# Two FFN stages: the first unit's product P6 goes between P1 and P2, and the second unit's first low block is computed on VectorE

## Chip, cores and metric

One core of a Trainium2 chip runs the whole program. The metric is the device time of one execution in microseconds (us); of the kernel before, three runs and one profiled execution are shown. Less is better.

## What is computed

One layer of a hybrid decoder trunk on 512 tokens of width 1024, in float32: a half-step SwiGLU FFN, a token mixer (dilated attention beside an mLSTM), and a second half-step FFN, each between RMSNorms.

```
def swiglu(x, w_gate, w_up, w_down):
    return (jax.nn.silu(x @ w_gate) * (x @ w_up)) @ w_down
...
x = x + 0.5 * rmsnorm(swiglu(rmsnorm(x, ffn1_pre_g), ...), ffn1_post_g)
x = x + rmsnorm(hybrid_mixer(rmsnorm(x, mix_pre_g), ...), mix_post_g)
x = x + 0.5 * rmsnorm(swiglu(rmsnorm(x, ffn2_pre_g), ...), ffn2_post_g)
```

D_FF is 2816, that is 22 blocks of 128 columns. The change touches only the first product pair of the two SwiGLU blocks, `x @ w_gate` and `x @ w_up`.

## The kernel before

**Precision.** A float32 matrix is split in a high part (a cast to float32r, done by ScalarE) and a low part (the matrix minus its high part). A product is the sum of high x high, high x low and low x high.

**Units.** In each FFN stage (tiles with _a in the first, _b in the second), the first three blocks of 128 columns (f = 0, 1, 2; `PLAIN = 3`) are done in the plain way. The 19 others are the units of `seven` (line 313). For each of them, gate and up weights together form a 2 x 2 matrix of blocks, as does the input, and the four block products are formed by seven, P1 to P7, with sums of blocks before and after (the Strassen-Winograd scheme). `product(out, k, ...)` (line 358) is P_k: twelve matmuls, eight high and four low for k of 1 and 2 (moving tile 128x256), four high (128x512) and four low (128x256) for the others. All lie on line 368 in the profile. The order of TensorE's products is written out by hand and chained (`pe`), and the `Order` object `do` (line 273) chains the instructions that go through it, engine by engine, in the order of the code. So an instruction of ScalarE, VectorE or GpSimd that waits holds up all that are chained behind it. These instructions all have line 279 in the profile.

**Accumulators.** Each unit has a PSUM tile `qa` (P1, then P2 added onto it) and a tile `qbc` of two banks: b takes P6, then P7 and P4, and c takes P5, then P3. P1 alone is needed too, so ScalarE copies it from `qa` to `q1` (in the profile q) before P2 is added. VectorE then reads the two banks in `outer` (with P6 and P5 in them, two additions into z and uv) before P7 and P3 are added, and in `inner` after them.

**Weights of a unit.** `load` (line 321) fetches gate and up weights as two tiles g and u of 512 KB from SP's queue, three buffers in turn for all of them. So the load of u of unit n+1 overwrites the buffer of g of unit n, and waits for the last reader of that. `sums` forms four sums of blocks on VectorE (ab and cd), `take` makes high and low parts:

- wh, the high part, is a cast on ScalarE, for pairs of blocks: (1, 2) is g itself, (6, 3) is cd, (7, 5) is ab, (4) is half of u.
- wl, the low part, is made in one of two ways. For sums it is a VectorE subtraction, which `take` returns as a function, to be called where its place is. For stored blocks, g and half of u, ScalarE writes the negated high part into wl, and an adding DMA from GpSimd's queue adds the stored block onto it.

`front` (line 343) is the `take` for (1, 2). The first unit's uses the subtraction, all others the adding DMA.

**The start of a stage.** Both first units are loaded and their `front` is called; the first unit's other parts follow at once. In the loop's first turn there is no unit before (`prev` is None), and the products come in this order: P1, P2, P6, P5 of the first unit, P1 of the second, then P7 and P3 of the first. ScalarE's copy to q1 stands after P1, its silu of `qa` after P2. In the following turns a unit has P1 (the second unit's is done already), P6, P5, then P4 of the unit before, P2, P7, P3.

Of the kernel before, what the change touches and what calls it, by code (L numbers as in the profile page):

```python
# [39 lines left out]
def tile_hybrid_block(ctx: ExitStack, tc: tile.TileContext, a: dict):  # L40
# [272 lines left out]
    def seven(do, fs, wgu, x, low, scr, pairs, aT, name, ahead):  # L313
# [3 lines left out]
        class Unit:  # L317
# [23 lines left out]
                do("gpsimd", "dma_start", wl, stored, accum_op=ADD)  # L341

            def front(self):
                if self.f > fs[0]:
                    return self.take((1, 2), self.gu[0], 2, self.stored(0))
                self.take((1, 2), self.gu[0])()

            def sums(self):
                g, u = self.gu
# [55 lines left out]
        us = [Unit(f) for f in fs] + [None, None]  # L405
        for u in us[:2]:
            u.load()
            u.front()
            if u is us[0]:
                u.sums()  # L410
                u.lowcd()
                u.take((4,), u.gu[1][:, 1:2, :], 1, u.stored(1)[:, 1:2, :])
                u.take((7, 5), u.ab)()
        prev = None
        for i in range(len(fs)):
            u, v, w = us[i:i + 3]
            if i != 1:
                u.open()
            if prev:
                prev.inner()  # L420
                prev.silu(1)
            if not v:
                next(ahead)
            if i != 1:
                u.product(u.a, 1, True, False)
                cast(u.q1, u.a)
            if not prev:
                u.product(u.a, 2, False, True)
                u.silu(0)
            u.product(u.b, 6, True, False)  # L430
            if w:
                w.load()
            if v:
                v.sums()
            u.product(u.c, 5, True, False)
            u.outer()
            if v:
                v.lowcd()
            if prev:
                prev.finish()  # L440
            if v:
                v.take((4,), v.gu[1][:, 1:2, :], 1, v.stored(1)[:, 1:2, :])
            if prev:
                u.product(u.a, 2, False, True)
            else:
                v.open()
                v.product(v.a, 1, True, False)
                cast(v.q1, v.a)
            if v:
                lowab = v.take((7, 5), v.ab)  # L450
            else:
                next(ahead)
            if prev:
                u.silu(0)
            if v:
                lowab()
            u.product(u.b, 7, False, False)
            u.product(u.c, 3, False, True)
            if w:
                w.front()  # L460
            prev = u
# [11 lines left out]
    def halves(v, n):  # L473
        return v.rearrange("p (a b) -> p a b", b=n)

    class Down:
# [81 lines left out]
        def cast(self, s, which):  # L558
            v = self.src[s][which == "w"]
            pool, tag, n = (wpool, "w", WMAX) if which == "w" or not self.xp else (self.xp, "x", T)  # L560
            n_ = v.shape[1] * v.shape[2]
            hl = [pool.tile([P, n], F32R, tag=f"{tag}{y}", bufs=5, name=f"{which}{y}{s}_{self.name}")[:, :n_] for y in "hl"]
            self.do("scalar", "copy", halves(hl[0], v.shape[2]), v)
            (self.w if which == "w" else self.x)[s] = hl
# [87 lines left out]
    def ffn(pool, todo, first_w, hT, wgu, wdq, wdh, wd, post, finish, name, begin=None, pins=(), aT=None):  # L652
# [23 lines left out]
        for f in range(EARLY, PLAIN):  # L676
# [5 lines left out]
            for b in range(2):  # L682
# [8 lines left out]
        pairs = pctx.enter_context(tc.tile_pool(name=f"pairs_{name}", bufs=2, space=bass.MemoryType.PSUM,  # L691
                                                reuse_waits="tile"))
        last = seven(do, range(PLAIN, NF), wgu, x, low, scr, pairs, aT, name, ahead)
        dn = ExitStack()
        next(ahead)
# [1146 lines left out]
```

## Time and profile before

| what | value |
|---|---|
| median of three runs | 1310.59 us (1307.78 to 1311.33) |
| profiled execution, its own time | 1308.08 us |
| its span, from the first to the last instruction | 1306.3 us |
| granted TensorE clock | 0.999 |
| TensorE matmul busy | 1293.5 us, 99% of the span |
| VectorE busy | 1041.2 us, 80% |
| ScalarE busy | 722.8 us, 55% |
| GpSimd busy | 188.5 us, 14% |
| first FFN stage: starts of the first and last matmul of line 368 | 46.5 us and 240.3 us |
| second FFN stage: the same | 1003.2 us and 1195.8 us |

In the rows of the profile PE is TensorE's matmuls, PEld its weight loads, DVE is VectorE, ACT ScalarE, POOL GpSimd and SP the engine whose queue issues the loads. A row of a timeline has the start in us from the start of the span, the duration, engine, line, operation, output and inputs, the number of instructions merged in it, and in brackets the idle time of the engine before it and what ended that. Ends of matmuls are modelled, so the difference of two starts is the better measure of a product's length. The times of the runs and of the profiled execution are those of the whole execution, a little longer than the span.

### The profile page before, as it was taken

To read this page: it belongs to the slowest core of one execution; us is meant where nothing else is said; L and a number is where in the kernel's file an instruction comes from. 1 tells how busy PE (TensorE), PEld (TensorE's weight loads), DVE (VectorE), ACT (ScalarE), POOL (GpSimd) and SP (SyncE) were. 2 spreads that over 40 slices of the span, in tenths; PEclk is the share of its full clock that TensorE was granted. 3 is DMA by queue.
4 is the path that set the end of the run, shared out by engine and by line. 5 is a ranking of instruction groups with operands and counts; after the bars stand their busy time and mean duration, and the time that the engine had idled before them with its cause. 6 is when DMAs were issued, how large, how long until landed. Compare 5 with 4: busy or idle time off the path is not lost.

```text
span 1306.3 us, 19592 instructions
## 1 busy us (share of the span) xinstructions
PE 1293.5 (99%) x7413; PEld 1137.4 (87%) x7413; DVE 1041.2 (80%) x1601; ACT 722.8 (55%) x1139; POOL 188.5 (14%) x249
## 2 busy tenths in 40 slices
PE   9999999999999999999999999999999999999997
PEld 8899999888898888888888889999888999998886
DVE  7799998889894577576798687676388999998887
ACT  6566666566644546435565554434265666665663
POOL 1111111221302110011112010000010111111220
PEclk9999999999999999999999999999999999999999
DMA  5587888697468963257637532335414778876981
GB/s 196 127 200 181 185 193 187 179 241 157 149 174 191 327 129 116 73 159 177 218 90 179 169 97 65 98 113 162 162 61 110 192 176 191 193 178 176 271 171 65
DMA packets 62766, 211.49 MB, mean 162 GB/s; under 512 B 7316, under 2 KB 8364, under 8 KB 62416
## 3 DMA queue, kind: packets, MB, share of 16 engines
q0 software_dynamic: 29824, 94.06, 34.5%
q1 hardware_dynamic: 32832, 116.18, 27.2%
q8 instruction: 58, 0.95, 0.3%
q14 instruction: 36, 0.29, 0.1%
q10 hardware_dynamic: 16, 0.00, 0.0%
HBM read 200.70 MB, written 9.46 MB: 161 GB/s over the span
## 4 chain that ended last, share of the span: by engine, by line
PE 93%; issue 3%; DVE 2%; DMA 1%; ACT 1%; POOL 0%; POOLq 0%; DVEq 0%; ACTq 0%
PE qbc_b L368 10%; PE qbc_a L368 10%; PE pq L204 8%; PE pm L204 7%; PE qa_b L368 4%; PE qa_a L368 4%; PE qb_gm L1262 4%; PE acc_o L259 3%; PE accb_b L584 3%; PE vo1p L993 3%; PE w12p L993 3%; PE vo0p L993 3%; PE accb_a L584 3%; PE accc_b L584 2%; PE accc_a L584 2%
## 5 line engine op out<-in xcount | busy, mean ns | idle before, releaser
L368 PE MATMUL qbc_b<-x_b,wh_b 128*128 128x512 f32 x304 | 83.1, 395 | 0.0
L368 PE MATMUL qbc_a<-x_a,wh_a 128*128 128x512 f32 x304 | 83.1, 395 | 0.0
L204 PE MATMUL pq<-hT_mx,wh_qk 128*128 128x512 f32 x320 | 76.9, 392 | 0.0
L204 PEld LDWEIGHTS pq<-hT_mx,wh_qk 128*128 128x128 f32 x320 | 59.4, 188 | 12.0
L204 PE MATMUL pm<-hT_mx,wh_mqk 128*128 128x512 f32 x256 | 61.3, 392 | 0.0
L368 PEld LDWEIGHTS qbc_b<-x_b,wh_b 128*128 128x128 f32 x304 | 52.1, 189 | 7.0
L368 PEld LDWEIGHTS qbc_a<-x_a,wh_a 128*128 128x128 f32 x304 | 52.1, 189 | 7.0
L279 POOL DMA_DIRECT2D wl_a<-in_wgu x37 | 32.2, 869 | 176.8 <-ACT wl_a L279 144.3
L279 POOL DMA_DIRECT2D wl_b<-in_wgu x37 | 31.5, 851 | 173.1 <-ACT wl_b L279 135.4
L204 PEld LDWEIGHTS pm<-hT_mx,wh_mqk 128*128 128x128 f32 x256 | 47.4, 188 | 9.5
L368 PEld LDWEIGHTS qbc_b<-x_b,wl_b 128*128 128x128 f32 x304 | 46.6, 188 | 6.5
L368 PEld LDWEIGHTS qbc_a<-x_a,wl_a 128*128 128x128 f32 x304 | 46.6, 188 | 6.5
L368 PE MATMUL qbc_a<-x_a,wl_a 128*128 128x256 f32 x304 | 48.2, 280 | 0.0
L368 PE MATMUL qbc_b<-x_b,wl_b 128*128 128x256 f32 x304 | 48.2, 280 | 0.0
L368 PE MATMUL qa_a<-hT_f,wh_a 128*128 128x256 f32 x304 | 42.6, 283 | 0.7 <-ACT q_a L279 0.7
L368 PE MATMUL qa_b<-hT_f,wh_b 128*128 128x256 f32 x304 | 42.6, 283 | 0.5 <-ACT q_b L279 0.5
L114 DVE TENSOR_TENSOR wl_qk<-wf_qk,wh_qk 128x1024 fp32r<-128x1024 f32 x24 | 29.2, 1220 | 17.3 <-ACT wh_qk L98 9.3
L368 PEld LDWEIGHTS qa_a<-hT_f,wh_a 128*128 128x128 f32 x304 | 39.1, 190 | 1.0 <-ACT q_a L279 0.9
L368 PEld LDWEIGHTS qa_b<-hT_f,wh_b 128*128 128x128 f32 x304 | 39.1, 190 | 0.7 <-ACT q_b L279 0.7
L98 ACT CAST wh_qk<-wf_qk 128x1024 fp32r<-128x1024 f32 x24 | 25.0, 1046 | 26.3 <-PE pq L204 10.0
L204 PE MATMUL pq<-hT_mx,wl_qk 128*128 128x512 f32 x160 | 39.5, 389 | 0.0
L1170 DVE SCALAR_TENSOR_TENSOR z<-pm,cw,z 128x511 f32<-128x511 f32 (+2 forms) x48 | 35.3, 743 | 2.2 <-ACT z L1168 1.8
(955 smaller groups left out, 3855.2 us busy)
## 6 DMA issues: line engine op xcount, KB each, us to landing
wf_qk<-in_wqk SPq DMA_DIRECT2D x24, 512.0 KB, 4.4
g_a<-in_wgu SPq DMA_DIRECT2D x19, 512.0 KB, 5.4
u_a<-in_wgu SPq DMA_DIRECT2D x19, 512.0 KB, 5.4
g_b<-in_wgu SPq DMA_DIRECT2D x19, 512.0 KB, 5.5
u_b<-in_wgu SPq DMA_DIRECT2D x19, 512.0 KB, 5.2
wl_a<-in_wgu POOLq DMA_DIRECT2D x18, 512.0 KB, 5.6
wl_b<-in_wgu POOLq DMA_DIRECT2D x18, 512.0 KB, 5.6
wf_mqk<-in_wmqk SPq DMA_DIRECT2D x16, 512.0 KB, 4.3
```

Source lines behind the costliest of these rows:

```text
L98: return nc.scalar.copy(wh, wf)
L114: last_low[0] = nc.vector.tensor_tensor(wl[:, :m], wf[:, :m], wh[:, :m].bitcast(F32), op=ALU.subtract).ins
L204: nc.tensor.matmul(out, lhsT=wt[:, k * P:(k + 1) * P], rhs=x[:, k, 0:T], start=n == 0, stop=n == len(terms) - 1)
L259: nc.tensor.matmul(out, lhsT=x[:, tk], rhs=w[:, cs], start=first and n == 0, stop=last and n == 2, skip_group_check=True)
L279: self.last[eng] = getattr(getattr(nc, eng), fn)(*args, **kw).ins
L368: i = nc.tensor.matmul(o, lhsT=w, rhs=v, start=first and n == 0, stop=last and n == len(terms) - 1, skip_group_check=True)
L584: nc.tensor.matmul(o, lhsT=x[:, tk], rhs=w[:, cs], start=k in "1256" and g + m + n == 0, stop=False, skip_group_check=True)
L993: nc.tensor.matmul(out[k][i], lhsT=x[:, 2 * g + m, i * P:(i + 1) * P], rhs=y[:, m * T:(m + 1) * T], start=k in "156" and g + m + j == 0, s ...
L1170: nc.vector.scalar_tensor_tensor(z[:, s:], src[:, :T - s], cw[:, ct, 3 - s:4 - s], z[:, s:], op0=ALU.mult, op1=ALU.add)
L1262: nc.tensor.matmul(out, lhsT=wt[:, i * P:(i + 1) * P], rhs=y[:, i, :], start=first and m == 0, stop=last and m == len(terms) - 1, skip_gro ...
```

## The change

In the first turn of the loop, P6 of the first unit goes between its P1 and P2. The second unit's low block for P1 and P2 is now computed like the first one's, by a VectorE subtraction; that subtraction is placed behind the second unit's four sums, ahead of P5 and of `outer`. From the third unit on, the adding DMA stays. Both FFN stages call the same function, so it is changed in both.

```
             def front(self):
-                if self.f > fs[0]:
+                if self.f > fs[1]:
                     return self.take((1, 2), self.gu[0], 2, self.stored(0))
-                self.take((1, 2), self.gu[0])()
+                return self.take((1, 2), self.gu[0])
...
         for u in us[:2]:
             u.load()
-            u.front()
+            second = u.front()
             if u is us[0]:
+                second()
                 u.sums()
                 u.lowcd()
...
             if i != 1:
                 u.product(u.a, 1, True, False)
                 cast(u.q1, u.a)
+            u.product(u.b, 6, True, False)
             if not prev:
                 u.product(u.a, 2, False, True)
                 u.silu(0)
-            u.product(u.b, 6, True, False)
             if w:
                 w.load()
             if v:
                 v.sums()
+            if not prev:
+                second()
             u.product(u.c, 5, True, False)
             u.outer()
```

More of the change, by code (lines that the diff above doesn't have):

```diff
@@ L343, in front @@
             def front(self):
-                if self.f > fs[0]:
+                if self.f > fs[1]:
                     return self.take((1, 2), self.gu[0], 2, self.stored(0))
-                self.take((1, 2), self.gu[0])()
+                return self.take((1, 2), self.gu[0])
             def sums(self):
@@ L407, in seven @@
             u.load()
-            u.front()
+            second = u.front()
             if u is us[0]:
+                second()
                 u.sums()
@@ L426, in seven @@
                 cast(u.q1, u.a)
+            u.product(u.b, 6, True, False)
             if not prev:
@@ L429, in seven @@
                 u.silu(0)
-            u.product(u.b, 6, True, False)
             if w:
@@ L434, in seven @@
                 v.sums()
+            if not prev:
+                second()
             u.product(u.c, 5, True, False)
```

## The prediction

> **What bounds the kernel now.** I read the page first (span, busy time, the row of granted clock, the chain that ended last by engine), then the list of TensorE's waits, then the timelines of the four engines round the places that this list names, and last the landing times of the loads there.
>
> ```profile
> span 1306.3 us, 19592 instructions
> ...
> PE 1293.5 (99%) x7413; PEld 1137.4 (87%) x7413; DVE 1041.2 (80%) x1601; ACT 722.8 (55%) x1139; POOL 188.5 (14%) x249
> ...
> PEclk9999999999999999999999999999999999999999
> ...
> PE 93%; issue 3%; DVE 2%; DMA 1%; ACT 1%; POOL 0%; POOLq 0%; DVEq 0%; ACTq 0%
> ```
>
> TensorE is busy for 99% of the span at the full granted clock, and the chain that ended last lies on it for 93%. A change pays here only if it shortens TensorE's work or takes out a wait of TensorE.
>
> ```profile
> PE qa_a L368 <- DMA wl_a<-in_wgu: 2.0, 1, 2.0
> ...
> PE qa_b L368 <- DMA wl_b<-in_wgu: 1.0, 1, 1.0
> PE qa_a L368 <- ACT q_a L279: 0.7, 1, 0.7
> PE qa_b L368 <- ACT q_b L279: 0.5, 1, 0.5
> ```
>
> This list (total, times, longest) holds four waits at the change's place, once in each of the two FFN stages (tiles _a and _b): on ScalarE's copy q, and on the landing of the adding DMA into wl. The only others in it lie in the opening of the kernel. So nearly all that can be won is here.
>
> The first FFN stage on TensorE (start, duration, instruction; brackets: idle time and what ended it):
>
> ```profile
> 46.52 1.11 PE L368 MATMUL qa_a<-hT_f,wh_a 128*128 128x256 f32 x8
> ...
> 48.86 1.22 PE L368 MATMUL qa_a<-hT_f,wh_a 128*128 128x256 f32 x8 [0.75 <-ACT q_a L279]
> ...
> 50.40 1.09 PE L368 MATMUL qbc_a<-x_a,wh_a 128*128 128x512 f32 x4
> ...
> 52.73 0.64 PE L368 MATMUL qbc_a<-x_a,wl_a 128*128 128x256 f32 x4
> 53.21 1.12 PE L368 MATMUL qa_a<-hT_f,wh_a 128*128 128x256 f32 x8
> 56.28 0.74 PE L368 MATMUL qa_a<-hT_f,wl_a 128*128 128x256 f32 x4 [1.96 <-DMA wl_a<-in_wgu]
> 56.86 1.08 PE L368 MATMUL qbc_a<-x_a,wh_a 128*128 128x512 f32 x4
> ...
> 59.65 1.09 PE L368 MATMUL qbc_a<-x_a,wh_a 128*128 128x512 f32 x4
> ...
> 65.30 1.19 PE L368 MATMUL qbc_a<-x_a,wh_a 128*128 128x512 f32 x4
> ```
>
> In the code's names: P1 of the first unit (start 46.52), P2 of it (48.86), P6 (50.40), P5 (to 53.21), P1 of the second unit (53.21, its low part held until 56.28), P7 of the first unit (56.86), P3 up to 59.65, then the second unit; 65.30 is the second unit's P7. Now the chain that ended last, start and duration:
>
> ```profile
> 48.86 7.38 DMA wl_a<-in_wgu
> ...
> 78.25 1.44 PE qa_a L368 x12
> ```
>
> The first row says that the adding DMA itself, 7.38 us from issue to landing, carried the path. The second is one undisturbed product into qa, twelve matmuls in 1.44 us. P6 and P5 together take 53.21 - 50.40 = 2.81 us. From P1 to P7 the first stage has three qa products and these two: 3 x 1.44 + 2.81 = 7.13 us of work. It takes 56.86 - 46.52 = 10.34 us. **3.21 us are lost there**, a little more than the listed idle times (0.75 + 1.96), since the first matmul after a stall is longer and the modelled ends overlap.
>
> The second FFN stage on TensorE:
>
> ```profile
> 1003.22 1.11 PE L368 MATMUL qa_b<-hT_f,wh_b 128*128 128x256 f32 x8
> ...
> 1005.27 1.22 PE L368 MATMUL qa_b<-hT_f,wh_b 128*128 128x256 f32 x8 [0.46 <-ACT q_b L279]
> ...
> 1009.62 1.12 PE L368 MATMUL qa_b<-hT_f,wh_b 128*128 128x256 f32 x8
> ...
> 1012.36 1.09 PE L368 MATMUL qbc_b<-x_b,wh_b 128*128 128x512 f32 x4
> ```
>
> Likewise 1012.36 - 1003.22 = 9.14 us, less 7.13: **2.01 us are lost**. Both stages together lose 5.22 us, the ceiling of the change.
>
> **The change, part by part.** ScalarE and VectorE in the first stage:
>
> ```profile
> 47.49 1.06 ACT L279 ACTIVATE wl_a<-wh_a 128x1024 fp32r<-128x1024 f32 x1
> 48.46 0.35 ACT L279 COPY q_a<-qa_a 128x256 f32<-128x256 f32 x1
> ```
>
> ```profile
> 39.03 1.22 DVE L279 TENSOR_TENSOR wl_a<-g_a,wh_a 128x1024 fp32r<-128x1024 f32 x1
> ...
> 44.43 1.23 DVE L279 TENSOR_TENSOR wl_a<-cd_a,wh_a 128x1024 fp32r<-128x1024 f32 x1 [0.51 <-ACT wh_a L279]
> 46.55 1.22 DVE L279 TENSOR_TENSOR wl_a<-ab_a,wh_a 128x1024 fp32r<-128x1024 f32 x1 [0.90 <-ACT wh_a L279]
> ...
> 50.34 0.68 DVE L279 TENSOR_TENSOR ab_a<-u_a 128x512 f32<-128x512 f32 x1
> 53.48 0.69 DVE L279 TENSOR_TENSOR z_a<-qbc_a,q_a 128x512 f32<-128x512 f32 x1 [2.46 <-PE qbc_a L368]
> 54.20 0.69 DVE L279 TENSOR_TENSOR uv_a<-qbc_a,z_a 128x512 f32<-128x512 f32 x1
> ...
> 61.18 0.68 DVE L279 TENSOR_TENSOR ab_a<-g_a,u_a 128x512 f32<-128x512 f32 x1
> ...
> 64.55 0.69 DVE L279 TENSOR_TENSOR uv_a<-qbc_a,z_a 128x512 f32<-128x512 f32 x1
> ```
>
> (1) The first unit's P6 moves between P1 and P2. P2 adds to the bank that ScalarE must first copy to q, and that copy started only at 48.46, because the negating pass (1.06 us from 47.49) stood before it in the queue. P6 lasts 1.40 us (half of 2.81), the copy 0.35, so P2 finds the copy done. P6 would start at 46.52 + 1.44 = 47.96 instead of 50.40: its low weights are written by 44.43 + 1.23 = 45.66, and its bank is of another tile than qa. P5 would start at 47.96 + 1.40 + 1.44 = 50.80; its weights are ready at 46.55 + 1.22 = 47.77. Nothing is added to any queue. This takes out the wait on q, with its slower first matmul.
>
> (2) The second unit's low block no longer takes ScalarE's negating pass and the adding DMA. Removed: one pass of 1.06 us on ScalarE, one issue on GpSimd's queue, 512 KB of traffic. None of these is on TensorE, but their end, the landing, was the wait at 56.28. What stood behind the pass on ScalarE was the copy to q, which now starts as soon as P1 ends.
>
> (3) Added: one VectorE subtraction of 128x1024. The row at 39.03 is the same instruction for the first unit: 1.22 us. It is queued behind the second unit's four sums, the last of which ends at 50.34 + 0.68 = 51.02, and ends at 52.24. TensorE asks for it at the low part of the second unit's P1, which now starts at 46.52 + 7.13 - 1.44 + 0.96 = 53.17 (0.96 is the high part's length before the low part in an undisturbed product, two thirds of 1.44). Cover 0.93 us. Behind the subtraction on VectorE stands the first outer addition, which before started 53.48 - 53.21 = 0.27 us after P5's last issue, so now at 52.21 + 0.27 = 52.48, 0.24 us after the subtraction ends: it fills idle time and costs nothing. Were that cover gone, TensorE would pay for VectorE's lateness one for one, by the next point.
>
> (4) What is late next: P7 of the first unit adds to the banks that the outer additions read, and it must wait for them. That this wait is real shows at 65.30, where the second unit's P7 starts 0.06 us after the addition of 64.55 ends (65.24), its first matmuls 0.10 longer than those at 50.40 (1.19 against 1.09). The additions end 54.20 + 0.69 - 53.21 = 1.68 us after P5's last issue. Between P5 and P7 stands only the second unit's P1, 1.44 us. So P7 waits 1.68 + 0.06 - 1.44 = 0.30 us, and loses 0.10 more: **0.40 us**, which the longer stall hid before. The bounds: 0 if the overlap lets P7 start anyway, 1.3 if the addition is held by a subtraction twice as long (1.22 - 0.24 = 0.98 more on the 0.30). I take 0.40, the rows' own value. In the second stage:
>
> ```profile
> 1006.51 0.68 DVE L279 TENSOR_TENSOR ab_b<-u_b 128x512 f32<-128x512 f32 x1
> ...
> 1010.61 0.69 DVE L279 TENSOR_TENSOR uv_b<-qbc_b,z_b 128x512 f32<-128x512 f32 x1
> ```
>
> The additions end at 1010.61 + 0.69 = 1011.30, again 1.68 us after 1009.62, so 0.40 there too; the subtraction would end at 1006.51 + 0.68 + 1.22 = 1008.41, 0.77 before the addition (1008.91 + 0.27).
>
> (5) Moved: the SP queue's load of u for the third unit. It overwrites the buffer of the second unit's g, whose last reader becomes the new subtraction.
>
> ```profile
> 50.48 0.33 SPq L325 DMA_DIRECT2D u_a<-in_wgu  x1
> ```
>
> ```profile
> 1006.65 0.33 SPq L325 DMA_DIRECT2D u_b<-in_wgu  x1
> ```
>
> In the first stage it goes out at 52.24 + 0.06 = 52.30 instead of 50.48, in the second at 1008.47 instead of 1006.65; the next g load stands behind it on SP, and waits for ScalarE at about that time anyway. VectorE reads u in the third unit's sums, which stood at 61.18, 4.32 us after the first unit's P7. With P7 at 56.86 - 2.81 (point 6) these sums fall at 58.37: 6.07 us for the landing. In the second stage P7 falls at 1012.36 - 1.61, the sums at 1015.07: 6.60 us. Landings (minimum, median, maximum): u loads of the first stage, its g loads, and the one u load of 1006.65 alone:
>
> ```profile
> DMA to landing us min/median/max: 3.6/5.4/5.7
> ...
> DMA to landing us min/median/max: 4.0/5.4/7.3
> ...
> DMA to landing us min/median/max: 6.9/6.9/6.9
> ```
>
> A load takes 5.4 us in the middle, and at most 5.7 for u of the first stage, so I cost this at nothing. The cover that hides it is 0.4 to 1.2 us. If it is gone, the sums are late, the outer additions of the second unit with them, and its P7, which already has no slack at 65.30, pays one for one. The 6.9 and the 7.3 were in the crowd with the adding DMA that is now removed.
>
> [...]
>
> (6) **The sum.** First stage 3.21 - 0.40 = 2.81 us, second 2.01 - 0.40 = 1.61 us, together 4.4 us. The rest of the program has no wait of TensorE that could give it back, and its transfers start on releases that move along. The profiled execution had 1308.08 us around its span of 1306.3, so 1303.7 for it. It lay 2.5 us below the median of the runs shown (1310.59), which gives **1306.2 us**.
>
> **The rivals.** (A) The load of u lands late. For it: its cover shrinks from 61.18 - 50.48 = 10.7 to 6.1 us, and rows of 6.9 and 7.3 exist; against it: half a megabyte less in its way. At 6.9 us it costs 0.83 + 0.30 = 1.1 us, at 7.3 us 1.23 + 0.70 = 1.9 us: a gain of 2.5 to 3.3 us, 1307.3 to 1308.1 us.
>
> (B) The same load, much later, so that the stall returns in the second unit: slower than before. It decides from a landing of 6.07 + 2.81 = 8.9 us in the first stage and 6.60 + 1.61 = 8.2 in the second. At 10 us the loss is 3.9 + 3.4 = 7.3 us, 2.9 us slower net: 1313.5 us. Against it: none of the loads in these rows took over 7.3 us.
>
> (C) P7 does not wait: the whole 5.2 us, 1305.4 us. For it: the span between the addition's end and 65.30 is only 0.06 us; against it: that same row's longer first matmuls.
>
> (D) The time is not kept: TensorE is earlier, but some later transfer paces it and gives the stall back. Then about 1310.6 us. Against it: the list of TensorE's waits names no such transfer; it could name one only once TensorE is early.
>
> **How the numbers follow.** Forecast 0.55, A 0.22, B 0.04, C 0.10, D 0.09. The measurement can tell 0.3%, 3.9 us, from no change; the forecast of 4.4 us is barely over it, and the runs shown spread over 3.5 us. Of the forecast's 0.55 I count 0.45 as faster, and all of C: 0.55. A, D and the remaining 0.10 are no change: 0.41. B is 0.04. The range goes from the lowest run less 5.2 us (1307.78 - 5.2 = 1302.6) to A with the highest run (1311.33 - 2.5, with some of D: 1309.2).
>
> **What would show it.** In the changed profile TensorE's waits on q and on wl's DMA are gone from both stages. P6 stands between the two qa products. A VectorE subtraction into wl from g stands behind the second unit's sums, about 1.2 us long, and P7 starts about 7.5 us after P1 in both stages, some 0.06 us after the second outer addition. The third unit's u load goes out some 1.8 us later. Wrong would be a new wait of TensorE in the second unit's P7, a wait of VectorE on the DMA of u, or a distance from P1 to P7 above 8 us; if these fit and the span does not fall by 4 us, the gain was given back later (D).

## The result, and the profile after

The changed kernel takes 1303.88 us (median of six runs, 1303.61 to 1306.36) against 1310.96 us before (six runs, 1307.78 to 1314.18): a ratio of 0.9949, interval 0.9933 to 0.9965. That is faster by 6.7 us (4.6 to 8.8); 4.4 were forecast. The profiled execution was the longest of the six, 1306.36 us. (In the experiments e6 and e7 below, one run each stood at over twice the time; it is left out of their medians and ranges.)

From the page, the span and busy time; then TensorE's waits (total, times, longest):

```profile
span 1304.5 us, 19588 instructions
...
PE 1293.7 (99%) x7413; PEld 1137.4 (87%) x7413; DVE 1043.8 (80%) x1603; ACT 720.5 (55%) x1137; POOL 186.3 (14%) x247
```

```profile
PE w12p L996 <- ACT v12flat L1027: 2.1, 1, 2.1
...
PE qbc_a L368 <- DVE uv_a L279: 0.2, 1, 0.2
```

The four waits at the change's place are gone, and two new ones stand in the list: 0.2 us behind the outer additions (uv), and 2.1 us in the mixer, at the w12p products. The first FFN stage on TensorE:

```profile
46.53 1.12 PE L368 MATMUL qa_a<-hT_f,wh_a 128*128 128x256 f32 x8
...
47.97 1.09 PE L368 MATMUL qbc_a<-x_a,wh_a 128*128 128x512 f32 x4
...
49.37 1.11 PE L368 MATMUL qa_a<-hT_f,wh_a 128*128 128x256 f32 x8
...
50.80 1.09 PE L368 MATMUL qbc_a<-x_a,wh_a 128*128 128x512 f32 x4
...
52.20 1.11 PE L368 MATMUL qa_a<-hT_f,wh_a 128*128 128x256 f32 x8
53.15 0.64 PE L368 MATMUL qa_a<-hT_f,wl_a 128*128 128x256 f32 x4
53.94 1.20 PE L368 MATMUL qbc_a<-x_a,wh_a 128*128 128x512 f32 x4 [0.15 <-DVE uv_a L279]
...
55.45 1.09 PE L368 MATMUL qbc_a<-hT_f,wh_a 128*128 128x512 f32 x4
```

P6 starts at 47.97, P2 at 49.37 without a wait, P5 at 50.80, P1 of the second unit at 52.20 with its low part following at once at 53.15. Only P7 (53.94) waits, with a longer first row (1.20). P3 starts at 55.45, 8.92 us after P1. P3 in the two stages of the kernel before:

```profile
58.25 1.09 PE L368 MATMUL qbc_a<-hT_f,wh_a 128*128 128x512 f32 x4
...
1013.76 1.09 PE L368 MATMUL qbc_b<-hT_f,wh_b 128*128 128x512 f32 x4
```

There it started 58.25 - 46.52 = 11.73 us after P1. VectorE and SP's load of u for the third unit:

```profile
50.97 1.22 DVE L279 TENSOR_TENSOR wl_a<-g_a,wh_a 128x1024 fp32r<-128x1024 f32 x1
52.47 0.69 DVE L279 TENSOR_TENSOR z_a<-qbc_a,q_a 128x512 f32<-128x512 f32 x1 [0.29 <-PE qbc_a L368]
53.20 0.69 DVE L279 TENSOR_TENSOR uv_a<-qbc_a,z_a 128x512 f32<-128x512 f32 x1
...
58.39 0.68 DVE L279 TENSOR_TENSOR ab_a<-g_a,u_a 128x512 f32<-128x512 f32 x1
```

```profile
52.21 0.33 SPq L325 DMA_DIRECT2D u_a<-in_wgu  x1
```

The new subtraction runs at 50.97 for 1.22 us, the outer additions follow at 52.47 and 53.20, and the third unit's sums begin at 58.39 with no idle time before them. The load of u was thus in time; the trace has no record of its landing. The second FFN stage on TensorE (P1 and P3), and its load of u with the landing:

```profile
1002.93 1.11 PE L368 MATMUL qa_b<-hT_f,wh_b 128*128 128x256 f32 x8
...
1011.85 1.09 PE L368 MATMUL qbc_b<-hT_f,wh_b 128*128 128x512 f32 x4
```

```profile
1008.06 0.33 SPq L325 DMA_DIRECT2D u_b<-in_wgu  x1
```

```profile
DMA to landing us min/median/max: 3.9/3.9/3.9
```

The load landed after 3.9 us, against 6.9 before. P1 to P3 is 8.92 us here too; before it was 1013.76 - 1003.22 = 10.54 us. So the two stages gave 11.73 - 8.92 = 2.81 us and 10.54 - 8.92 = 1.62 us, **4.4 us together**. The spans differ by 1306.3 - 1304.5 = 1.8 us only. The other 2.6 us were lost in the mixer in this execution, at the same products of w12p; first before, then after:

```profile
415.16 1.07 PE L993 MATMUL w12p<-wh_w,part 128*128 128x512 f32 x4
...
416.52 1.10 PE L993 MATMUL w12p<-wh_w,hT_mx 128*128 128x512 f32 x4
```

```profile
412.27 1.07 PE L996 MATMUL w12p<-wh_w,part 128*128 128x512 f32 x4
...
415.91 1.44 PE L996 MATMUL w12p<-wh_w,hT_mx 128*128 128x512 f32 x4 [2.12 <-ACT v12flat L1027]
```

Before, the second row shown starts 1.36 us after the first; after, it starts 3.64 us later, and its own matmuls are longer (1.44 against 1.10). What is late are the adding DMAs into v_x. The changed kernel on GpSimd, which issues them, and on ScalarE, which casts v_x:

```profile
398.83 0.86 POOL L965 DMA_DIRECT2D wf_w<-in_wv  x1 [33.29 <-DMA wf_w<-in_wv]
400.15 0.85 POOL L965 DMA_DIRECT2D wf_w<-in_wv  x1 [0.47 <-issue]
400.69 1.21 POOL L977 DMA_DIRECT2D v_x<-in_wv  x1
```

```profile
410.80 1.05 ACT L270 CAST wh_w<-v_x 128x1024 fp32r<-128x1024 f32 x1 [6.65 <-DMA v_x<-in_wv]
414.33 1.04 ACT L270 CAST wh_w<-v_x 128x1024 fp32r<-128x1024 f32 x1 [2.48 <-DMA v_x<-in_wv]
```

GpSimd could issue the first DMA into v_x only at 400.69, behind two into wf_w, the first of which had waited until 398.83 for a load into the same tile. ScalarE's cast of v_x waited 6.65 us for the landing, the next cast another 2.48 us for the next DMA into v_x, and the copy that frees w12p's bank (v12flat, at 415.28) stood behind both. The kernel before, on GpSimd:

```profile
399.00 0.85 POOL L962 DMA_DIRECT2D wf_w<-in_wv  x1 [30.16 <-DMA wf_w<-in_wv]
```

The DMA that leads this queue went out at nearly the same time in both, although TensorE was 2.8 us earlier after the change.

So one execution shows a gain of 1.8 us, the medians one of 7, and the stages 4.4. The experiments look for the difference.

### The profile page after: what moved, and what is told of

Read it like the earlier page. It is cut to its first block, busy times and chain, and to the rows that moved or that the text cites. A ratio compares the mean times of both kernels' runs of the same rounds, so it can differ in the third digit from the quotient of the medians.

```text
span 1304.5 us, 19588 instructions
## 1 busy us (share of the span) xinstructions
PE 1293.7 (99%) x7413; PEld 1137.4 (87%) x7413; DVE 1043.8 (80%) x1603; ACT 720.5 (55%) x1137; POOL 186.3 (14%) x247
## 4 chain that ended last, share of the span: by engine, by line
PE 97%; DVE 1%; DMA 1%; ACT 0%; issue 0%; POOL 0%; DVEq 0%; POOLq 0%; ACTq 0%
PE qbc_b L368 10%; PE qbc_a L368 10%; PE pq L204 8%; PE pm L204 7%; PE qa_a L368 4%; PE qa_b L368 4%; PE qb_gm L1265 4%; PE acc_o L259 3%; PE accb_b L587 3%; PE vo1p L996 3%; PE vo0p L996 3%; PE accb_a L587 3%; PE w12p L996 2%; PE accc_b L587 2%; PE accc_a L587 2%; PE pg_a L218 2%
```

## The experiments

Two kinds were run: parts of the change (e1, e2, e5), and what differs between executions (e3, e4, and e6 to e11); e12 joins what gave something. All ratios are against runs of the kernel before on the same chip.

| kernel | median us | lowest to highest us | ratio (interval) |
|---|---|---|---|
| e1 P6 moved only | 1311.97 | 1307.82 to 1313.87 | 1.0005 (0.9990 to 1.0019) |
| e2 low block on VectorE only | 1305.99 | 1305.30 to 1306.34 | 0.9963 (0.9949 to 0.9976) |
| e3 the changed kernel again | 1304.57 | 1303.78 to 1305.02 | 0.9950 (0.9932 to 0.9968) |
| e4 the kernel before again | 1310.91 | 1308.67 to 1313.52 | 1.0000 (0.9987 to 1.0014) |
| e5 P2 behind P5 | 1303.12 | 1302.87 to 1303.97 | 0.9933 (0.9920 to 0.9946) |
| e6 v_x ahead of wf_w | 1303.81 | 1303.65 to 1305.00 | 0.9940 (0.9926 to 0.9955) |
| e7 before, waits filled | 1309.33 | 1307.37 to 1314.36 | 0.9986 (0.9973 to 0.9999) |
| e8 late subtraction | 1308.73 | 1307.02 to 1312.95 | 0.9983 (0.9971 to 0.9994) |
| e9 e8 with e6's order | 1308.18 | 1306.88 to 1309.88 | 0.9980 (0.9966 to 0.9993) |
| e10 e9, half filled | 1307.13 | 1306.81 to 1307.35 | 0.9973 (0.9960 to 0.9985) |
| e11 e9, filled | 1307.15 | 1306.88 to 1307.90 | 0.9972 (0.9959 to 0.9984) |
| e12 e5 and e6 together | 1303.15 | 1302.89 to 1304.29 | 0.9941 (0.9919 to 0.9962) |

**e1: P6 between P1 and P2, and nothing else.**

```
+            u.product(u.b, 6, True, False)
             if not prev:
                 u.product(u.a, 2, False, True)
                 u.silu(0)
-            u.product(u.b, 6, True, False)
```

> The old kernel with P6 between P1 and P2 and nothing else; the second unit's low block still comes from the adding DMA. Theory (the landing of that DMA sets the first unit's P7): the landing does not move, so P2 no longer waits for the copy to q, but the second unit's P1 waits that much longer; P1 to P7 stays 10.3 us in the first and 9.1 us in the second FFN stage, and the time is that of the kernel before within 1 us. Rival (the two waits add up, each is worth its own length): P1 to P7 falls by 1.0 us in the first and 0.7 us in the second stage, 1.7 us in all.

TensorE's waits of this kernel:

```profile
PE qa_a L368 <- DMA wl_a<-in_wgu: 3.7, 1, 3.7
PE qa_b L368 <- DMA wl_b<-in_wgu: 2.3, 1, 2.3
```

The wait on q is gone, and the wait on the adding DMA grew from 2.0 to 3.7 us and from 1.0 to 2.3 us. The time is that of the kernel before. This half shows no gain by itself: it moves the wait one product on.

**e2: the low block on VectorE, with P2 in its old place.**

> The changed kernel with P6 back behind P2; only the low block on VectorE is kept. Theory: the copy to q now starts when P1 ends (48.2 us instead of 48.46 in the first stage) but P2 still waits for it, about 0.7 us in each stage, and P7 still pays 0.4 us for the outer additions; P1 to P7 is 7.13 + 0.7 + 0.4 = 8.2 us in both stages, so 2.1 us and 0.9 us less than before, 3.0 us in all: 1.4 us slower than the whole change. Rival (without the negating pass in front of it the copy is hidden, and P6's move is worth nothing): 7.5 us in both stages, the time of the whole change.

```profile
46.60 1.12 PE L368 MATMUL qa_a<-hT_f,wh_a 128*128 128x256 f32 x8
...
48.66 1.22 PE L368 MATMUL qa_a<-hT_f,wh_a 128*128 128x256 f32 x8 [0.46 <-ACT q_a L279]
...
54.74 1.20 PE L368 MATMUL qbc_a<-x_a,wh_a 128*128 128x512 f32 x4
```

P2 waits 0.46 us for the copy, and P1 to P7 is 54.74 - 46.60 = 8.14 us (8.2 expected; 8.14 in the second stage too). The median is 1.4 us above e3's, as expected. P6's move is worth that, once the DMA is gone; alone (e1) it is worth nothing that these runs can show.

**e3 and e4: both kernels once more.**

> The changed kernel once more. Two stories for the 7 us between the medians, of which the two FFN stages of the profiles show 4.4. Story 1 (the mixer): a wait of 0 to 3 us at the w12p products, behind the adding DMA into v_x, comes and goes from one execution to the next and was mostly absent in the runs after. Then the profiles of this kernel show P1 to P7 at 7.4 us in both stages each time, and spans that differ by that wait alone (1301.9 without it, 1304.5 with 2.6 us). Story 2 (the stages): the old kernel's adding DMA mostly lands later than in the one profile, so its stalls were 2 to 3 us longer than 5.2 and the change is worth 7: then the mixer's wait is the same in the mean of both kernels.

> The kernel before once more, as a measure of how it differs from itself. Ratio 1.000 within 0.2%. Story 1 (the mixer): P1 to P7 again 10.3 and 9.1 us within 0.5, and if the execution is longer than 1308.1 us, a wait of TensorE at the w12p products or elsewhere in the mixer that the first profile did not have. Story 2 (the stages): P1 to P7 longer than 10.3 and 9.1 us by 2 to 3 us together, with a landing of the adding DMA above 7.4 and 6.7 us.

e3's profile has the stages as in the first profile of the changed kernel (P1 to P7 7.41 us in both) and a wait of 0.3 us at w12p; its time is 1304.69 us. There the DMA that leads GpSimd's queue went out at 396.77 instead of 398.83. Neither of the two stories in these expectations holds for e4. Its stalls are no longer than in the first profile (P1 to P7 10.26 us in the first stage, and 8.38 us in the second, where 9.1 was expected), its list of waits names none in the mixer, and yet something else is there. TensorE behind the wait of the first stage, and the same time by windows (columns: window, length, busy us and count of PE, PEld, DVE, ACT, POOL, then granted clock, with 1 for full speed, DMA share and GB/s):

```profile
56.07 0.74 PE L368 MATMUL qa_a<-hT_f,wl_a 128*128 128x256 f32 x4 [1.88 <-DMA wl_a<-in_wgu]
56.65 1.72 PE L368 MATMUL qbc_a<-x_a,wh_a 128*128 128x512 f32 x4
...
61.00 1.08 PE L368 MATMUL qbc_a<-x_a,wh_a 128*128 128x512 f32 x4
```

```profile
56.00:60.00 4.00, 3.93 (x15) 3.40 (x16) 1.23 (x1) 2.88 (x4) 0.00 (x0) 0.61 0.63 174
60.00:64.00 4.00, 4.00 (x24) 3.50 (x23) 2.70 (x5) 0.96 (x2) 0.85 (x1) 0.96 0.36 52
```

Behind the wait of 1.88 us (and one of 0.8 before it) P7's first four matmuls take 1.72 us, not 1.09, and the granted clock falls to 0.61 and 0.96 in two windows of 4 us. In e1's profile a whole window, 56 to 60 us, reads 0.50, and P7's four low matmuls, from 59.80, take 1.05 us (0.63 at full clock in e3, at 55.11); in e4 they take 1.05 us too, at 58.17. At 0.50 the stretch is (0.39 + 0.04) x 4 / 0.5 = 3.4 us long, an estimate from the two windows. P7 and P3 took 61.00 - 56.65 = 4.35 us in it, against 59.65 - 56.86 = 2.79 us in the first profile, so it cost 1.6 us. e1's profile has twice as long a stretch, (0.50 + 0.36) x 4 / 0.5 = 6.9 us by its windows of 56 to 60 us (0.50) and 60 to 64 us (0.64). The window before them reads 1.00, so the clock fell at about 56 us, some 1 us before the wait of 3.65 us ended (57.07), when TensorE had been idle for about 2.6 us. The first profile of the kernel before, with nearly the same wait as e4 (1.96 us), had no such stretch (1.00 from 56 to 64 us).

That gave a third story: **the stall costs its own length, and in some executions the clock behind it.** The records of 89 runs of the kernel before (the three groups of runs shared by the experiments, and e4), by their mean granted clock: 28 at 0.999 with a mean of 1308.97 us, 28 at 0.998 with 1310.73, 21 at 0.997 with 1312.19, 9 at 0.996 with 1313.45, and three lower; the mean of all is 1310.90. A step of 0.001 is 1.3 us of 1305; between these means lie 1.3 to 1.8 us. The clock is not all that varies: the runs at 0.999 alone spread from 1306.60 to 1310.79 us, and e4's profiled run, at 0.997, took 1308.67. (The third decimal is rounded, so 0.998 beside 0.999 says little by itself: some of the shortest runs of e5 and e6 stand at 0.998. Two of the three lower records, 0.947 with 1312.04 and 1312.07 us, do not fit their times at all.) Of e1's twelve runs, with the longest waits, eight stand at 0.997 or 0.996. All twelve runs of the changed kernel (its first six and e3's) stand at 0.999, with a mean of 1304.37.

**e5: P2 behind P5.**

```
             u.product(u.b, 6, True, False)
-            if not prev:
-                u.product(u.a, 2, False, True)
-                u.silu(0)
...
             u.product(u.c, 5, True, False)
+            if not prev:
+                u.product(u.a, 2, False, True)
+                u.silu(0)
             u.outer()
```

> The changed kernel with the first unit's P2 (and the silu after it) moved behind P5: P1, P6, P5, P2, P1 of the second unit, P7. Theory (P7 waits for the outer additions, 0.4 us in each stage): P5 now ends 1.4 us earlier, the additions stand right behind the new subtraction on VectorE and end before P7 is due; P1 to P7 is 7.13 us instead of 7.41 in both stages, and the longer first matmul is gone: 0.8 us less than the changed kernel. Rival (the subtraction then delays the additions): they start 1.2 us late, and P7 waits as before, no change.

```profile
46.40 1.11 PE L368 MATMUL qa_a<-hT_f,wh_a 128*128 128x256 f32 x8
...
53.52 1.10 PE L368 MATMUL qbc_a<-x_a,wh_a 128*128 128x512 f32 x4
...
54.92 1.08 PE L368 MATMUL qbc_a<-hT_f,wh_a 128*128 128x512 f32 x4
```

P1 to P7 is 7.12 us and P1 to P3 8.52, 0.40 less than in the changed kernel: the term for P7 was right, and it can be had back. The median is 0.8 us below that of the changed kernel's first six runs and 1.4 below e3's; the intervals overlap, so it is the profile that shows it.

**e6: the mixer's order.**

```
-                with tc.issue_after(chain[1]) if behind else nullcontext():
+                with tc.issue_after(chain[1]):
                     nc.gpsimd.dma_start(f7[g], block("u0", g), accum_op=ADD)
```

> The changed kernel with one order more in the mixer: the adding DMA into wf_w is queued on GpSimd behind the first two adding DMAs into v_x, which the w12p products need sooner. Theory (the wait of 0 to 2.6 us at w12p comes from v_x standing behind wf_w in GpSimd's queue): v_x lands some 2 us earlier, TensorE does not wait at w12p, and no run is longer than the shortest by more than 1 us; the median is that of the changed kernel or up to 1 us less. Rival (v_x lands late because of traffic): the wait stays.

```profile
398.22 0.86 POOL L977 DMA_DIRECT2D v_x<-in_wv  x1 [32.53 <-DVE wl_w L271]
...
403.25 1.87 POOL L965 DMA_DIRECT2D wf_w<-in_wv  x2
```

```profile
405.14 1.05 ACT L270 CAST wh_w<-v_x 128x1024 fp32r<-128x1024 f32 x1 [1.07 <-PE w12p L996]
```

The first DMA into v_x now goes out at 398.22 instead of 400.69, its cast runs at 405.14 instead of 410.80, and no wait at w12p is listed; nor is one in the profiles of e9 to e12, which have this order too. Without it e8 has 2.3 us, e3 0.3 us, e2 and e5 none that is listed. So the order in GpSimd's queue takes the wait out. How it does so is shown in part only: the earlier issue gives 2.5 us of the 5.7 by which the cast is earlier; the rest is a shorter time from issue to cast (6.9 us instead of 10.1), and here the transfers into wf_w no longer go just ahead. The rival, traffic, is thus not excluded as a part of the cause. The highest run is 1305.00, not 1304.65 as expected, and the median hardly moves, as it would if the wait is small in most executions.

**e7: the kernel before, its waits filled with needless matmuls.**

```
...
+                    if idle and n == 8:
+                        pe[:] = [i.ins]
+                        self.idle(idle)
...
```

> The kernel before, with 4 needless matmuls into a spare bank while P2 waits for the copy, and 11 more while the second unit's P1 waits for the adding DMA; they compute nothing that is used. The waits stay as long as they are (10.3 and 9.1 us from P1 to P7), but TensorE is idle for less of them. Theory (an idle stretch now and then makes the throttle grant half the clock for 3.4 or 6.8 us, as seen after the stall in two of the profiles, and that is what the kernel before loses beyond 4.4 us): the granted clock is 0.999, no run is above 1309.5 us, the median is 1308.3 us, 2 us less than before. Rival (the spread of the kernel before comes from the mixer or from late landings): median and spread are those of the kernel before, 1310.3 us, runs up to 1314.

Half met. The ratio is below 1 by barely more than its interval. Six of ten runs stand at 0.999 (5 of the 23 runs of the kernel before beside them) and two at 0.998, but two are at 0.997 with 1313.46 and 1314.36 us. The stalls did not stay as long as expected either: in the profile, P1 to P7 is 9.44 and 9.47 us, not 10.3 and 9.1. The wait depends on a landing, which I can't hold still, and fillers can also run into the work (in the first stage the low part starts at 55.47 right behind them, with no wait listed). So this run does not separate the clock from the length of the stall. Where the clock fell in these two runs stays open, since they have no trace.

**e8: a stall without the DMA.** The new subtraction goes behind the outer additions.

```
-            if not prev:
-                second()
             u.product(u.c, 5, True, False)
             u.outer()
+            if not prev:
+                second()
```

> The changed kernel with the new VectorE subtraction behind the first unit's outer additions instead of ahead of them. No adding DMA comes back, but the low part of the second unit's P1 now waits for VectorE, about 1.9 us in both stages, and P7's wait of 0.4 goes. So P1 to P7 is about 9.0 us in both stages, 3 us in all above the changed kernel. Theory (idle time itself makes the throttle act, whoever causes it): the runs spread again, from 1307 to 1312 us, and some profile or runs have a granted clock below 0.999. Rival (the throttle reacts to something of the adding DMA): all runs within 1 us of 1307. The u load goes out 2.8 us later than in the changed kernel, at 55.1 us; if it takes 5.4 us, VectorE waits for it by under 1 us before the third unit's sums, and the second unit's P7 pays that too.

TensorE's waits, and windows of the second stage (columns as above):

```profile
PE qa_b L368 <- DVE wl_b L279: 1.8, 1, 1.8
PE qa_a L368 <- DVE wl_a L279: 1.8, 1, 1.8
```

```profile
1014.00:1018.00 4.00, 3.03 (x14) 2.78 (x15) 2.95 (x3) 2.26 (x3) 0.55 (x1) 0.81 0.86 211
1018.00:1022.00 4.00, 4.00 (x19) 3.41 (x19) 2.21 (x4) 1.48 (x3) 0.86 (x1) 0.76 0.54 138
```

TensorE waits 1.8 us for VectorE in each stage, and the clock falls to 0.81 and 0.76 behind the second of them, with no adding DMA at fault; at 0.50 that is (0.19 + 0.24) x 4 / 0.5 = 3.4 us. Behind the first it does not fall (P7's first matmuls take 1.09 us, at 55.66). In the mixer it fell too (0.89 and 0.68 in two windows of 4 us), after a wait of 2.3 us at w12p. One expectation missed: the load of u went out at 52.88 us, not 55.1, and the next load of g at 55.06, just as the late subtraction had ended. The two loads had evidently changed buffers, so this run does not test a late u.

**e9, e10, e11: the same stall, idle, half filled and filled.** e9 is e8 with e6's order, so that no other wait is left. e10 and e11 put 7 and 15 needless matmuls in the stall.

> A clean stall: the changed kernel with the new subtraction behind the outer additions (TensorE idle for 1.76 us in each FFN stage, no adding DMA involved) and the mixer's order of the previous study, so that TensorE waits nowhere else. Theory (idle time makes the throttle act in some executions): the lowest run near 1307 us, the median 1 to 2 us above it, mean granted clocks of 0.998 and below in most of the runs, single runs up to 1311 us. Rival (the spread belonged to the mixer's wait): all runs within 1 us of 1307, clocks 0.998 to 0.999.

> The same stall, of the same length, with 7 needless matmuls into a spare bank in it, so that TensorE is idle for about 1.0 us instead of 1.76. Theory: fewer or no runs with a lowered clock, median 0.5 to 1.5 us below the clean stall, lowest run the same 1307 us. Rival: the times of the clean stall.

> The same stall filled with 15 needless matmuls (1.8 us), so that TensorE is hardly idle. Nothing else differs: every other instruction runs at the same place. Theory: no run with a lowered clock; all runs within 1 us of 1307 us, the median 1 to 2 us below the clean stall. Rival (the stall alone, not idleness, costs the time): median and spread of the clean stall.

TensorE round the stall in the three:

```profile
52.18 1.11 PE L368 MATMUL qa_a<-hT_f,wh_a 128*128 128x256 f32 x8
55.05 0.74 PE L368 MATMUL qa_a<-hT_f,wl_a 128*128 128x256 f32 x4 [1.76 <-DVE wl_a L279]
```

```profile
53.26 1.00 PE L363 MATMUL spare_a<-hT_f,wh_a 128*128 128x256 f32 x7
55.18 0.74 PE L379 MATMUL qa_a<-hT_f,wl_a 128*128 128x256 f32 x4 [0.92 <-DVE wl_a L279]
```

```profile
53.37 1.96 PE L363 MATMUL spare_a<-hT_f,wh_a 128*128 128x256 f32 x15
55.29 0.74 PE L379 MATMUL qa_a<-hT_f,wl_a 128*128 128x256 f32 x4
```

The low part of P1 starts 2.87 us after the high part in all three (for e10 and e11: 55.18 - 52.31 and 55.29 - 52.42), so the stall has one length; TensorE's idle time in it is 1.76, 0.92 and about 0 us. The twelve runs of e9 have a mean of 1308.04 us and spread over 3.0 us, seven of them at a clock of 0.998 or 0.997. Those of e10 have 1307.12 and spread over 0.5 us, those of e11 1307.23 and 1.0 us. In e10 nothing is longer than the rest by a lowered stretch's 1.6 us. So idleness alone costs 0.9 us in the mean (1308.04 - 1307.12), and 0.92 us of it in a stage did no such harm here. e9's profile is of a run at full clock (0.999); the lowered stretch itself is seen behind this stall in e8. With that, the third story is shown for this stall. For the kernel before, it is borne out by its runs and by e4 and e1, not shown.

**e12: e5 and e6 together.**

> The changed kernel with P2 behind P5 and with the adding DMA into wf_w behind the first two into v_x in the mixer. TensorE then waits neither in the FFN stages nor at w12p. By the rows: 0.8 us below the changed kernel for the order of the products, and whatever the mixer's wait took (0 to 2.6 us, mostly under 1): median 1302.9 us, ratio to the kernel before 0.993, no run above 1304 us.

The median is 1303.15 us (1302.9 expected), the ratio 0.9941 (0.993 expected), and one run, the profiled one, stands above 1304 us, at 1304.29. No wait is left in the FFN stages or at w12p, but the list has one of 0.5 us elsewhere in the mixer (line 1128, on VectorE). The median is 0.7 and 1.4 us below the changed kernel's two medians, within the intervals, and no better than e5 alone.

## Why the prediction was right, and where its size came short

The numbers in brackets are the forecast ones.

- **P6 ahead of P2 (1).** As forecast: P6 at 47.97 (47.96), P5 at 50.80 (50.80), no wait on q. What the prediction did not say is that this half shows no gain without the other (e1).
- **The adding DMA and its subtraction (2, 3).** As forecast: subtraction at 50.97 (51.02), additions at 52.47 (52.48), no wait in P1.
- **P7 late next (4).** Forecast 0.40 us per stage; measured 8.92 against 8.52 us in e5, 0.40.
- **The load of u (5).** Issued at 52.21 (52.30) and 1008.06 (1008.47). The landing is on record for the second stage only: 3.9 us (4.0 in e3) instead of the 5.4 taken from the median row, inside its 6.60; it lies near the shortest of the first stage's u loads before, 3.6. In the first stage the sums show only that it came in time. Rivals A and B did not come.
- **The sum (6).** 2.81 + 1.61 forecast, 2.81 + 1.62 measured in the profiles. The median is 1303.88 us (1306.2).
- **What was mis-sized** is the same term, the removed stall. It was priced by its length in one profile whose granted clock was full (0.999). In a part of the executions of the kernel before, the clock was also lowered: 33 of the 89 records stand at 0.997 or less, and in e4's profile the stretch lies behind the stall. The prediction's rows could not show that, and the gain beyond 4.4 us is nothing that it foresaw. At equal clock, 0.999, both kernels differ by 1308.97 - 1304.37 = 4.6 us, the forecast; over all runs by 1310.90 - 1304.37 = 6.5 us. The 1.9 us between go with the clock. That the clock can fall at an idle stall was shown with another stall, in e8 (0.81 and 0.76 behind 1.76 us), and that its idleness costs time in e9 to e11 (0.9 us in the mean); that this accounts for the 1.9 us of the kernel before is not shown, as e7 settled it only in part and the stalls also differ in length between executions (P1 to P7 of the second stage 9.14 and 8.38 us). 1.76 us of idle time were enough behind one of e8's two stalls, and the lowered stretch was 3.4 us long there as in e4, by their windows.
- **Rival D** was real in the profiled execution: the mixer gave 2.6 us back. The prediction named the possibility and not the place. Its sentence that the other transfers start on releases that move along failed there: the DMA that leads GpSimd's queue moved by 0.2 us (399.00 to 398.83) when TensorE moved by 2.8. In e3 it moved by 2.2 us (396.77); why not in the other execution stays open. Most runs did not pay: the lowest, 1303.61, is the profiled before less 4.5.

## What to carry to other kernels

Price a stall of the matmul engine by its length and by what the clock does around it: here the lowered stretch in e4 cost 1.6 us beside the wait of 1.88. One profile at full clock does not show that, so look at the clocks of many runs, and at a kernel's spread as a sign (3.0 us in e9, 0.5 in e10). Removing one of two waits in a row can be worth nothing until the other goes: P6's move gave a ratio of 1.0005 alone (e1), and 1.4 us once the DMA was gone (e2 against e3). Before a lead is counted, look at the next place where a queue (here GpSimd's) holds a transfer that does not move along with it.

## What was not expected of the hardware

The granted clock fell at waits of 1.76 to 3.65 us: it read 0.50 over 56 to 60 us in e1, and at 0.50 the windows give a stretch of 6.9 us there and of 3.4 us in e4 and in e8. It did so in some executions and not in others of the same kernel (in e4 at 1.88 us, not in the first profile before at 1.96), and in e8 behind one of two equal waits of one execution. Counted back at 0.50 from the windows of 4 us, it fell about 0.8 us after the wait's end in e4 (60 - 0.39 x 4 / 0.5 = 56.88 against 56.07), about 1.5 us after it in e8 (1018 - 0.19 x 4 / 0.5 = 1016.48 against 1014.97), and about 1 us before it in e1 (56 against 57.07). With 0.92 us of idle time instead of 1.76 in the same stall, none of twelve runs stood 1.6 us above the rest (e10, a spread of 0.5 us). In e8's execution the clock fell behind a wait of 2.3 us at w12p (0.89 and 0.68), and in that of the changed kernel it did not behind one of 2.1 us (1.00 from 412 to 424 us).
